# Holding a rotation's copies behind products, and a nearer norm broadcast, in a two-layer hybrid block

## The chip, the cores and the metric

One core of a Trainium2 chip runs the kernel. The metric is the device time of one execution in microseconds. All times below are from the kernel before: its timed runs and one profiled execution.

## What is computed

Two layers over 512 tokens of width 1024, in float32. Each layer projects the normalised input to many parts, mixes them in three branches, and adds a feed-forward part and a gated part:

```python
h = rms_norm(x, g_pre_mix)
q, k, v, qi, ki, wi, xr, gr, zu, zv, gate_logits = jnp.split(h @ w_in, offsets, axis=-1)
q, k, qi, ki = (apply_partial_rope(a, positions, 16) for a in (q, k, qi, ki))   # written out one by one
y_a = dsa_attention(q, k, v, qi, ki, wi)     # scores of qi, ki, wi select 128 keys of 512
y_b = rg_lru(causal_depthwise_conv(xr, ...), ...) * gelu(gr)
y_c = chunked_spatial_gating(gelu(zu), rms_norm(gelu(zv), g_gmlp_v), ...)
merged = jnp.einsum('bsnd,nbsd->bsd', sigmoid(gate_logits), branches_of(y_a, y_b, y_c))
x = x + rms_norm(merged @ w_out, g_post_mix)
x = x + rms_norm(square(relu(rms_norm(x, g_pre_ffn) @ w_ffn_up)) @ w_ffn_down, g_post_ffn)
x = x + rms_norm((p_i @ w_ple) * sigmoid(x @ w_ple_gate), g_post_ple)
```

`apply_partial_rope` is the rotation: it turns the first 16 of each head's 64 columns by the position.

## The kernel before

**Products.** Every float32 product is made of three with the operands split in a high and a low part (`mm3`, L298 to L300; L590 in `tokens`; L356 in `gemm_arriving`): `wh` by `xh`, `wl` by `xh`, `wh` by `xl`. The 303 weight tiles of 128x1024 come by DMA from the SP queue. `prep` makes `wh` with a cast on ScalarE (ACT, L243) and `wl` with a subtraction on VectorE (DVE, L244), three tiles ahead of TensorE (PE) and with four buffers each. A tile is 24 products of 512 columns.

**Rotations.** `rope` takes a projection from PSUM: on DVE a multiplication (L573) and a shuffle (L574), then on GpSimd (POOL) a multiplication (L575) and an addition (L576). What follows a rotation is the split of its result: `ki_split`, `stacked` (L650 on ACT, L651 on DVE, in pairs) for `qi` and `k`, `q_split` (L1026, L1028 on ACT, L1027 on DVE) for `q`. `xc_split` (L616 on ACT, L617 on POOL) does the same for the convolution's result, which is not rotated.

**What sets the order.** The program is traced against a clock `clk` that only products advance (`tick`). `defer(us, fn)` puts `fn` on a list, and `run_later` traces it when the clock has passed `us` more microseconds. So `defer(TURN, ...)` traces a split 5 us of product time after its projection. Tasks on `idxq` (indexer: scores L681, then a selection of MAX8 and MATCH_REPLACE8, L714 and L716) and `attq` (attention) give their steps in the same way. Behind this the Tile framework's scheduler puts the instructions of each engine in order, by their dependencies. A copy can therefore land ahead of products or weight splits that were traced before it.

**Norms.** `rstd_tok` sums the squares with small products (L408), then DVE (L427) and POOL (L428) make 1/rms per token. `rstd_bc` spreads it over the partitions with transposes (L434). `Stats.row` and `Norm.complete` defer the first by 2.2 us after the last square and the second by 3.0 us more. In both layers `R`, the spread 1/rms, scales the projections; `x_tiles` uses it for the residual (L480 to L503).

**Attention.** `turn` transposes two blocks of the softmax's result (L953), splits them (L369 on ACT, L370 on DVE), and `values` multiplies them by V (L967).

Of the kernel before, what the change touches and what calls it, by code (L numbers as in the profile page):

```python
# [17 lines left out]
S = 512  # L18
# [27 lines left out]
def f32v(ap):  # L46
    return ap.bitcast(F32)
# [3 lines left out]
def hybrid_block_kernel(ctx, tc, xT, pT, pos, vec, bsp, freq, w_in, w_tok, w_lru, w_sp, w_br, w_out, w_up, w_dn, w_ple, w_gate, out, depth=DEPTH, dbg=None):  # L51
    nc = tc.nc
    V, A, G, PE = nc.vector, nc.scalar, nc.gpsimd, nc.tensor
# [13 lines left out]
    def tmp(dt=F32):  # L67
        return tp.tile([128, S], dt, tag="tmp", name=nm("tmp"), bufs=NTMP)
# [4 lines left out]
    def bank():  # L73
        return pp.tile([128, 512], F32, tag="ps", name=nm("ps"), bufs=8)

    def slot(tag, dt=F32, big=False):
        return cp.tile([128, 4, S] if big else [128, S], dt, tag=tag, name=nm(tag))
# [10 lines left out]
    TAIL = 3  # L88
    LEAD = 256
    ATT = 13  # L90
    TURN = 5
    WARM = 120
    FIRST = [0, 1, 4]

# [152 lines left out]
    def getw(key, ahead=LA):  # L247
        assert order[nget[0]][0] == key, (order[nget[0]][0], key)
        nget[0] += 1
        while nprep[0] < min(nget[0] + ahead, len(order)):  # L250
            prep()
        return prepared.pop(key)
# [8 lines left out]
    def defer(us, fn):  # L261
        later.append((clk[0] + us, uid[0], fn))
        uid[0] += 1

    def run_later(force=False):
        while later:
            later.sort(key=lambda e: e[:2])
            if not force and later[0][0] > clk[0]:
                return
            later.pop(0)[2]()  # L270

    def add_task(q, gen):
        q["wait"].append(gen)
# [17 lines left out]
    def finish(q):  # L291
        run_later(force=True)
        while q["act"] or q["wait"]:
            tick(0.3)
# [7 lines left out]
    def gemm(ps, w, xs, kk, c0=0, st=None, r=FULL):  # L302

        h3, l3 = [v.rearrange("p (k c) -> p k c", k=kk) for v in w]
        for k in range(kk):
            if st is not None and k == kk - 2:
                st.partial()
            mm3(ps, h3[:, k, c0:c0 + 128], l3[:, k, c0:c0 + 128], xs[k][0][:, r], xs[k][1][:, r], k == 0, k == kk - 1)
            tick(0.65 * width(r) / S)
# [67 lines left out]
    class Stats:  # L377
# [59 lines left out]
        def row(self, div, dst):  # L437


            def complete(r):  # L440
                def tok():
                    self.rstd_tok(div, r)
                    defer(3.0, lambda: A.copy(dst[:, r], self.rstd_bc(r)))

                defer(2.2, tok)

            return complete

    class Norm:
# [6 lines left out]
        def complete(self, r):  # L456
            def tok():
                self.st.rstd_tok(self.div, r)
                defer(3.0, bc)

            def bc():
                self.gens[r.start] = self.tiles(r, self.st.rstd_bc(r))

            defer(2.2, tok)
# [68 lines left out]
    for l in range(depth):  # L533
        vc = vecs[l]

        def col(c):
            return vc[:, c:c + 1]
# [18 lines left out]
        def proj(name, ahead=LA):  # L556
            ps = bank()
            gemm(ps, getw(("in", l, name), ahead), XS, KT)
            return ps
# [11 lines left out]
        def rope(ps, n=128):  # L571
            t1, u = tmp(), tmp()
            V.tensor_mul(t1[:n], ps[:n], Cr[:n])  # L573
            V.stream_shuffle(u[:n], ps[:n], mask=SHUF)  # L574
            G.tensor_mul(u[:n], u[:n], Sr[:n])  # L575
            G.tensor_add(t1[:n], t1[:n], u[:n])  # L576
            return t1
# [19 lines left out]
        idxq = {"wait": [], "act": [], "max": 1}  # L597
# [5 lines left out]
        for j in range(4):  # L603
            ps = first[j]
            xr = tmp()
            V.tensor_mul(xr, ps, R)
            xc = slot(f"M{4 + j}")
            A.activation(xc, xr, AF.Identity, bias=col(V_CB + j), scale=col(V_CW + 12 + j))
            for i in range(3):
                s = 3 - i  # L610
                V.scalar_tensor_tensor(xc[:, s:], xr[:, :S - s], col(V_CW + 4 * i + j), xc[:, s:], op0=ALU.mult, op1=ALU.add)
            xh, xl = slot(f"B{j}", F32R), slot(f"B{4 + j}", F32R)
            XC.append((xc, xh, xl))

            def xc_split(xc=xc, xh=xh, xl=xl):
                A.copy(xh, xc)  # L616
                G.tensor_sub(xl, xc, f32v(xh))  # L617

            defer(10 + 5 * j, xc_split)


        ps = proj("ki")
# [5 lines left out]
            A.copy(kih[64:128], kf[0:64])  # L628
            A.copy(kil[64:128], f32v(kil[0:64]))

        defer(TURN, ki_split)
        wf = tmp()
        A.copy(wf, ps)
        WI = small(32, "wi", 2).rearrange("p (t h) -> p t h", t=4)
# [5 lines left out]
            for t in range(1, 4):  # L640
                V.tensor_scalar(WI[:, t, :], pw[:, t * 128 + 64:t * 128 + 72], rt[:, t:t + 1], IDX_SCALE, op0=ALU.mult, op1=ALU.mult)

        defer(9, wi_turn)

        def stacked(f, q0, q1):


            for s, q in enumerate((q0, q1)):
                r, other = slice(64 * s, 64 * s + 64), slice(64 - 64 * s, 128 - 64 * s)
                A.copy(q[r], f[r])  # L650
                V.tensor_sub(q[other], f[r], f32v(q[r]))  # L651
            return q0, q1

        QI = []
        for j in range(4):
            ps = proj(f"qi{j}")
            QI.append((slot(f"A{j}", F32R), slot(f"A{4 + j}", F32R)))
            defer(TURN, lambda f=rope(ps), q=QI[j]: stacked(f, *q))

        def qk(a, b, c, d, jobs):  # L660

# [23 lines left out]
        def scores(t, sc):  # L685
            n = 128 * (t + 1)
            qs = slice(t * 128, (t + 1) * 128)
            for j in range(4):
                pr = qk_full(QI[j], kih, kil, t, n)
                for s in range(2):  # L690
                    rl = tmp()
                    A.activation(rl[:, :n], pr[s][:, :n], AF.Relu)
                    w = WI[:, t, 2 * j + s:2 * j + s + 1]
                    if j == 0 and s == 0:
                        V.tensor_scalar(sc[:, :n], rl[:, :n], w, None, op0=ALU.mult)
                    else:
                        V.scalar_tensor_tensor(sc[:, :n], rl[:, :n], w, sc[:, :n], op0=ALU.mult, op1=ALU.add)
                yield 3.4
            V.tensor_add(sc[:, qs], sc[:, qs], tri)

        def indexer():
            sc = {t: tmp() for t in (1, 2, 3)}
            for t in (1, 2, 3):
                yield from scores(t, sc[t])
            for t in (1, 2, 3):
                yield from select(t, sc[t])
# [23 lines left out]
            G.tensor_scalar(BIAS[t], gt[:, :n], -NEG, NEG, op0=ALU.mult, op1=ALU.add)  # L730
            yield 1.0

        defer(9, lambda: add_task(idxq, indexer()))


        bs = tmp()
# [23 lines left out]
        for j in range(4):  # L760
            ps = proj(f"zu{j}")
# [16 lines left out]
        for j in range(4):  # L778
# [3 lines left out]
            for hf in range(2):  # L782
                ps = bank()
# [4 lines left out]
                for s in range(2):  # L788
                    r = slice(64 * s, 64 * s + 64)
# [55 lines left out]
        for j in range(4):  # L845
# [7 lines left out]
            r, i = tmp(), tmp()  # L853
# [48 lines left out]
        def gated(n, ys, first=None, ds=range(8)):  # L902
            for d in ds:
                th = first if first is not None and d == 0 else gate(n, d)
                if d % 2 == 0:
                    w = getw(("br", l, n, d // 2), ahead=1)
                branch(n, d, w, ys, th)
# [5 lines left out]
        KK = [slot("K0", F32R, True), slot("K1", F32R, True)]  # L913
# [105 lines left out]
        for j in range(4):  # L1019
            f = rope(proj(f"q{j}"))  # L1020
            q2, ql = (slot(f"A{j}", F32R), slot(f"A{4 + j}", F32R)), tmp(F32R)

            def q_split(f=f, q2=q2, ql=ql):
                for s in range(2):
                    r, other = slice(64 * s, 64 * s + 64), slice(64 - 64 * s, 128 - 64 * s)
                    A.copy(q2[s][r], f[r])  # L1026
                    V.tensor_sub(ql[r], f[r], f32v(q2[s][r]))  # L1027
                    A.copy(q2[s][other], f32v(q2[s][r]))  # L1028

            defer(TURN, q_split)  # L1030
            Q.append((q2, ql))
            defer(TURN, lambda f=rope(proj(f"k{j}")), j=j: stacked(f, KK[0][:, j], KK[1][:, j]))
            if j == 0:
                finish(idxq)
            defer(ATT, lambda j=j: add_task(attq, attention(j)))
            gated(1, YB, ds=range(2 * j, 2 * j + 2))
# [23 lines left out]
        for d in range(5):  # L1060
            ps = bank()
# [8 lines left out]
        ps = bank()  # L1070
# [52 lines left out]
        for c in range(2):  # L1123
            w = getw(("ple", l, c), ahead=1)
            if c == 1:
                bc = st3.rstd_bc()
            for i in range(4):
                ps = bank()
# [14 lines left out]
        for d in range(5):  # L1143
            if d < 4:
                ps = first[d]
            else:
                ps = bank()
# [95 lines left out]
```

## Time and profile before

| | us |
|---|---|
| median of 3 runs | 1851.07 (1850.51 to 1853.98) |
| profiled execution | 1852.94 |
| its span in the profile | 1851.2 |
| PE busy | 1803.0 |
| DVE busy | 1159.5 |
| ACT busy | 800.3 |
| POOL busy | 361.6 |

Busy time is a mean over stages that differ: DVE's 63% holds a stretch of 120 us in which it hardly idles. PE's records overlap, since its products are pipelined: what counts is the distance from the start of one to the start of the next. A number in brackets at the end of a row is the idle time of the engine just before that instruction, with the instruction whose result ended it.

### The profile page before, as it was taken

The numbers are of one execution on the slowest core, as the hardware profiler recorded it, in microseconds if no ns is written. First come the engines' busy times: TensorE is split into PE (matmuls) and PEld (weight loads), VectorE is DVE, ScalarE is ACT, GpSimd is POOL, SyncE is SP. The second block draws the span as 40 slices with busy tenths as digits, with TensorE's granted clock in tenths as the row PEclk, the third lists the DMA queues.
The fourth block names the chain that finished last, engine by engine and source line by source line (L and its number), as shares of the span: only waits on it lengthen the run. The fifth ranks groups of instructions, "written<-read, shape, count | busy, mean of one in ns | idle before, by whom it ended". The sixth has DMA issues, their size and how long they took to land.

```text
span 1851.2 us, 22873 instructions
## 1 busy us (share of the span) xinstructions
PE 1803.0 (97%) x8798; PEld 1507.5 (81%) x8798; DVE 1159.5 (63%) x1939; ACT 800.3 (43%) x1292; POOL 361.6 (20%) x292
## 2 busy tenths in 40 slices
PE   8899999999999999999998999999999999999997
PEld 7787887888888888888887878877888888888886
DVE  6689996666386253533685999866563852544355
ACT  5466435664453322223455573455544432222233
POOL 3513212210240000003454141222004200000033
PEclk9999999999999999999999999999999999999999
DMA  5122322222223232332212223222222222222321
GB/s 173 63 92 85 98 92 91 69 80 82 90 80 108 97 98 96 99 106 91 92 58 97 68 92 103 91 80 72 89 80 92 92 92 101 96 97 97 108 80 58
DMA packets 49678, 167.77 MB, mean 91 GB/s; under 512 B 6048, under 2 KB 8864, under 8 KB 49568
## 3 DMA queue, kind: packets, MB, share of 16 engines
q1 hardware_dynamic: 47376, 163.64, 26.8%
q10 hardware_dynamic: 2192, 2.67, 0.4%
q8 instruction: 69, 1.13, 0.3%
q14 instruction: 41, 0.34, 0.1%
HBM read 164.19 MB, written 2.10 MB: 90 GB/s over the span
## 4 chain that ended last, share of the span: by engine, by line
PE 72%; DVE 12%; POOL 6%; issue 6%; ACT 4%; DMA 0%; SPq 0%; POOLq 0%; DVEq 0%; ACTq 0%
PE ps L298 21%; PE ps L299 20%; PE ps L300 20%; PE ps L356 3%; PE ps L590 3%; DVE wl L244 2%; POOL tmp L575 1%; POOL tmp L576 1%; DVE tmp L716 1%; DVE m L714 1%; POOL sacc L398 1%; POOL X L483 1%; PE ps L681 1%; PE ps L967 1%; DVE tmp L790 1%
## 5 line engine op out<-in xcount | busy, mean ns | idle before, releaser
L243 ACT CAST wh<-wr 128x1024 fp32r<-128x1024 f32 x303 | 316.6, 1049 | 453.3 <-PE ps L300 365.9
L244 DVE TENSOR_TENSOR wl<-wr,wh 128x1024 fp32r<-128x1024 f32 x303 | 386.8, 1280 | 188.7 <-ACT wh L243 188.0
L298 PE MATMUL ps<-xh,wh 128*128 128x512 f32 (+1 forms) x1296 | 502.7, 388 | 0.9 <-DVE tmp L370 0.9
L299 PE MATMUL ps<-xh,wl 128*128 128x512 f32 (+1 forms) x1296 | 495.5, 382 | 3.0 <-DVE wl L244 3.0
L300 PE MATMUL ps<-xl,wh 128*128 128x512 f32 (+1 forms) x1296 | 495.6, 382 | 0.0
L398 POOL TENSOR_TENSOR sacc<-sacc,tmp 128x256 f32<-128x256 f32 (+1 forms) x99 | 109.8, 1109 | 894.8 <-issue 584.5
L300 PEld LDWEIGHTS ps<-xl,wh 128*128 128x128 f32 x1296 | 243.9, 188 | 48.2
L299 PEld LDWEIGHTS ps<-xh,wl 128*128 128x128 f32 x1296 | 244.4, 189 | 47.1 <-DVE wl L244 3.9
L298 PEld LDWEIGHTS ps<-xh,wh 128*128 128x128 f32 x1296 | 244.0, 188 | 47.2 <-issue 1.9
L300 PE MATMUL ps<-V,wh 128*128 128x512 f32 (+1 forms) x528 | 195.4, 370 | 0.0
L298 PE MATMUL ps<-K,wh 128*128 128x512 f32 (+1 forms) x432 | 158.2, 366 | 0.0
L299 PE MATMUL ps<-K,wl 128*128 128x512 f32 (+1 forms) x432 | 157.8, 365 | 0.0
L300 PE MATMUL ps<-B,wh 128*128 128x512 f32 x336 | 130.9, 390 | 0.0
L298 PE MATMUL ps<-A,wh 128*128 128x512 f32 x320 | 125.0, 391 | 0.2 <-ACT A L369 0.2
L299 PE MATMUL ps<-A,wl 128*128 128x512 f32 x320 | 124.6, 389 | 0.0
L1102 DVE TENSOR_TENSOR M<-M,ps 128x512 f32<-128x512 f32 x48 | 33.0, 688 | 141.4 <-PE ps L300 141.4
L300 PEld LDWEIGHTS ps<-V,wh 128*128 128x128 f32 x528 | 99.5, 188 | 16.7
L1090 DVE TENSOR_TENSOR tmp<-ps,R 128x512 f32<-128x512 f32 x64 | 43.8, 690 | 108.6 <-PE ps L300 108.5
L356 PE MATMUL ps<-xl,wh 128*128 128x256 f32 (+1 forms) x264 | 88.1, 334 | 6.2 <-DVE xl L503 5.5
L298 PEld LDWEIGHTS ps<-K,wh 128*128 128x128 f32 x432 | 81.5, 189 | 13.3
L299 PEld LDWEIGHTS ps<-K,wl 128*128 128x128 f32 x432 | 81.5, 189 | 13.1
L356 PE MATMUL ps<-xh,wh 128*128 128x256 f32 (+1 forms) x264 | 87.1, 330 | 2.2 <-ACT xh L493 2.2
(237 smaller groups left out, 2733.0 us busy)
## 6 DMA issues: line engine op xcount, KB each, us to landing
wr<-in_w_in_dram SPq DMA_DIRECT2D x95, 512.0 KB, 3.3
wr<-in_w_up_dram SPq DMA_DIRECT2D x64, 512.0 KB, 3.3
wr<-in_w_dn_dram SPq DMA_DIRECT2D x64, 512.0 KB, 3.3
wr<-in_w_br_dram SPq DMA_DIRECT2D x24, 512.0 KB, 3.3
wr<-in_w_tok_dram SPq DMA_DIRECT2D x16, 512.0 KB, 3.3
wr<-in_w_out_dram SPq DMA_DIRECT2D x16, 512.0 KB, 3.3
wr<-in_w_gate_dram SPq DMA_DIRECT2D x16, 512.0 KB, 3.3
X<-in_xT_dram SPq DMA_DIRECT2D x8, 256.0 KB, 5.9
```

The costliest lines, as they stand in the source:

```text
L243: A.copy(hi, raw)
L244: V.tensor_sub(lo, raw, f32v(hi))
L298: PE.matmul(ps, wh, xh, start=start, stop=False)
L299: PE.matmul(ps, wl, xh, start=False, stop=False)
L300: PE.matmul(ps, wh, xl, start=False, stop=stop)
L356: PE.matmul(pss[o][:, r], (h3, l3, h3)[m][:, q], xs[q][m // 2][:, r], start=q == 0 and m == 0, stop=q == KT - 1 and m == 2)
L398: G.tensor_add(sacc[:, r], sacc[:, r], self.q[r.start, r.stop])
L483: (G if d in on_g else V).tensor_add(X[d][:, r], X[d][:, r], ys[d][:, r])
L575: G.tensor_mul(u[:n], u[:n], Sr[:n])
L590: PE.matmul(ps, x, w, start=k == 0 and i == 0, stop=k == KT - 1 and i == 2)
L1090: V.tensor_mul(t, ps, R)
L1102: V.tensor_add(F[d], F[d], ps)
```

## The change

Two numbers change and one is new: `TURN` 5 to 7, and `PICK` 1.7 in place of the 3.0 us between a norm's statistics and its broadcast. A new helper, `behind_products`, traces a function and gives each instruction that it made on ACT, DVE or POOL a dependency for the scheduler alone (no semaphore) on the last PE instruction traced before. `turn_later` is `defer` with that helper, and the splits behind rotations and `xc_split` use it. Some delays change: `xc_split` 10 to 12, `wi_turn` 9 to 14, the start of the indexer 9 to 12, and the statistics of the first half in `row` 2.2 to 8.0.

```diff
-    TURN = 5
+    TURN = 7
+    PICK = 1.7
...
+    def behind_products(fn):
+        ins = nc.cur_bb.bb.instructions
+        n0 = len(ins)
+        mark = next(i for i in reversed(ins[:n0]) if i.engine == mybir.EngineType.PE)
+        fn()
+        for i in nc.cur_bb.bb.instructions[n0:]:
+            if i.engine in (mybir.EngineType.Activation, mybir.EngineType.DVE, mybir.EngineType.Pool):
+                tc.add_manual_dep(i, mark.name, mybir.DependencyInfo(mybir.DependencyClass.NoSync, mybir.DependencyReason.SCHED_ONLY), reason="behind products")
+
+    def turn_later(us, fn):
+        defer(us, lambda: behind_products(fn))
...
-                    defer(3.0, lambda: A.copy(dst[:, r], self.rstd_bc(r)))
-                defer(2.2, tok)
+                    defer(PICK, lambda: A.copy(dst[:, r], self.rstd_bc(r)))
+                defer(2.2 if r.stop == S else 8.0, tok)
...
-                defer(3.0, bc)
+                defer(PICK, bc)
...
-            defer(10 + 5 * j, xc_split)
+            turn_later(12 + 5 * j, xc_split)
...
-        defer(TURN, ki_split)
+        turn_later(TURN, ki_split)
...
-        defer(9, wi_turn)
+        defer(14, wi_turn)
...
-            defer(TURN, lambda f=rope(ps), q=QI[j]: stacked(f, *q))
+            turn_later(TURN, lambda f=rope(ps), q=QI[j]: stacked(f, *q))
...
-        defer(9, lambda: add_task(idxq, indexer()))
+        defer(12, lambda: add_task(idxq, indexer()))
...
-            defer(TURN, q_split)
+            turn_later(TURN, q_split)
...
-            defer(TURN, lambda f=rope(proj(f"k{j}")), j=j: stacked(f, KK[0][:, j], KK[1][:, j]))
+            turn_later(TURN, lambda f=rope(proj(f"k{j}")), j=j: stacked(f, KK[0][:, j], KK[1][:, j]))
```

In the orders below the changed kernel's lines have other numbers: L244 is L245, L573 and L574 are L589 and L590, L575, L576 and L617 are L591, L592 and L633, L641 and L651 are L657 and L667, and L369, L1026, L1028 are L384, L1042, L1044.

On DVE in layer 0, behind the weight of the first tokens tile: `wl_129` (now `wl_128`), `wl_138` and `wl_151` are those of the second, third and fourth, and `A0` to `A7` are the rotated `qi`. Before (`wl_151` follows, behind the shuffle that belongs to the last row):

```order
L651 TENSOR_TENSOR A0_111_642<-tmp_113_644,A0_111_642 64x512
L651 TENSOR_TENSOR A4_112_643<-tmp_113_644,A4_112_643 64x512
L574 STREAM_SHUFFLE tmp_124_697<-ps_116_650 128x512
L244 TENSOR_TENSOR wl_129_706<-wr_127_703,wh_128_705 128x1024
L573 TENSOR_TENSOR tmp_132_741<-ps_126_702,tmp_73_523 128x512
L574 STREAM_SHUFFLE tmp_133_742<-ps_126_702 128x512
L651 TENSOR_TENSOR A1_121_694<-tmp_123_696,A1_121_694 64x512
L651 TENSOR_TENSOR A5_122_695<-tmp_123_696,A5_122_695 64x512
L244 TENSOR_TENSOR wl_138_751<-wr_136_748,wh_137_750 128x1024
L651 TENSOR_TENSOR A2_130_739<-tmp_132_741,A2_130_739 64x512
L651 TENSOR_TENSOR A6_131_740<-tmp_132_741,A6_131_740 64x512
L573 TENSOR_TENSOR tmp_141_786<-ps_135_747,tmp_73_523 128x512
```

Now:

```order
L245 TENSOR_TENSOR wl_128_693<-wr_126_690,wh_127_692 128x1024
L667 TENSOR_TENSOR A0_111_636<-tmp_113_638,A0_111_636 64x512
L667 TENSOR_TENSOR A4_112_637<-tmp_113_638,A4_112_637 64x512
L657 TENSOR_SCALAR wi_105_604<-ps_129_720,rt_37_283 128x8 x3
L589 TENSOR_TENSOR tmp_132_735<-ps_125_689,tmp_73_523 128x512
L590 STREAM_SHUFFLE tmp_133_736<-ps_125_689 128x512
L245 TENSOR_TENSOR wl_138_745<-wr_136_742,wh_137_744 128x1024
L667 TENSOR_TENSOR A1_120_681<-tmp_122_683,A1_120_681 64x512
L667 TENSOR_TENSOR A5_121_682<-tmp_122_683,A5_121_682 64x512
L589 TENSOR_TENSOR tmp_141_780<-ps_135_741,tmp_73_523 128x512
L590 STREAM_SHUFFLE tmp_142_781<-ps_135_741 128x512
L245 TENSOR_TENSOR wl_151_795<-wr_149_792,wh_150_794 128x1024
```

Each of the three weights stands ahead of one pair more than before, and the `wi` step, which stood ahead of the rows before, stands behind the first pair.

On POOL in the same place, up to the addition that ends the rotation of `qi1` (`tmp_123_696`, now `tmp_122_683`); `B4` to `B7` are the convolution's low parts. Before:

```order
L617 TENSOR_TENSOR B4_78_535<-M4_76_529,B0_77_534 128x512
L617 TENSOR_TENSOR B5_83_544<-M5_81_538,B1_82_543 128x512
L617 TENSOR_TENSOR B6_88_553<-M6_86_547,B2_87_552 128x512
L575 TENSOR_TENSOR tmp_100_595<-tmp_100_595,tmp_74_524 64x512
L576 TENSOR_TENSOR tmp_99_594<-tmp_99_594,tmp_100_595 64x512
L617 TENSOR_TENSOR B7_93_562<-M7_91_556,B3_92_561 128x512
L575 TENSOR_TENSOR tmp_114_645<-tmp_114_645,tmp_74_524 128x512
L576 TENSOR_TENSOR tmp_113_644<-tmp_113_644,tmp_114_645 128x512
L575 TENSOR_TENSOR tmp_124_697<-tmp_124_697,tmp_74_524 128x512
L576 TENSOR_TENSOR tmp_123_696<-tmp_123_696,tmp_124_697 128x512
```

Now:

```order
L591 TENSOR_TENSOR tmp_100_595<-tmp_100_595,tmp_74_524 64x512
L633 TENSOR_TENSOR B4_78_535<-M4_76_529,B0_77_534 128x512
L592 TENSOR_TENSOR tmp_99_594<-tmp_99_594,tmp_100_595 64x512
L591 TENSOR_TENSOR tmp_114_639<-tmp_114_639,tmp_74_524 128x512
L592 TENSOR_TENSOR tmp_113_638<-tmp_113_638,tmp_114_639 128x512
L633 TENSOR_TENSOR B5_83_544<-M5_81_538,B1_82_543 128x512
L591 TENSOR_TENSOR tmp_123_684<-tmp_123_684,tmp_74_524 128x512
L592 TENSOR_TENSOR tmp_122_683<-tmp_122_683,tmp_123_684 128x512
```

The low parts `B6` and `B7` moved behind the rotation of `qi1`, and `B5` behind that of `qi0`.

On ACT in layer 0, at the first `turn` of the attention (`tmp_547`, `tmp_550`, `tmp_561`) and the second `q` (`A1`, `A5`). Before:

```order
L1026 CAST A1_537_2636<-tmp_535_2630 64x512
L1026 CAST A5_538_2637<-tmp_535_2630 64x512
L369 CAST tmp_547_2664<-ps_546_2659 128x512
L1028 CAST A1_537_2636<-A1_537_2636 64x512
L1028 CAST A5_538_2637<-A5_538_2637 64x512
L243 CAST wh_558_2703<-wr_557_2701 128x1024
L369 CAST tmp_550_2690<-ps_549_2686 128x384
```

Now:

```order
L384 CAST tmp_547_2664<-ps_546_2659 128x512
L244 CAST wh_558_2697<-wr_557_2695 128x1024
L384 CAST tmp_550_2684<-ps_549_2680 128x384
L1042 CAST A1_537_2636<-tmp_535_2630 64x512
L1042 CAST A5_538_2637<-tmp_535_2630 64x512
L1044 CAST A1_537_2636<-A1_537_2636 64x512
L1044 CAST A5_538_2637<-A5_538_2637 64x512
```

The two splits of turned logits and a weight's cast stand ahead of the four copies of `q1`.

## Rows read from the trace of the kernel before

**Rows 1.** The page's first part: each engine's busy us, share of the span, instructions.

```profile
PE 1803.0 (97%) x8798; PEld 1507.5 (81%) x8798; DVE 1159.5 (63%) x1939; ACT 800.3 (43%) x1292; POOL 361.6 (20%) x292
```

**Rows 2.** PE's waits: who waited for what, us in total, times, longest.

```profile
PE ps L590 <- DVE wl L244: 10.5, 4, 4.2
...
PE ps L299 <- DVE wl L244: 4.4, 4, 1.5
PE ps L967 <- ACT tmp L369: 4.1, 4, 2.3
...
PE ps L967 <- DVE tmp L370: 1.7, 4, 0.9
...
PE ps L639 <- ACT tmp L633: 1.2, 2, 0.7
```

**Rows 3.** PE's timeline at the tokens of layer 0: start, us, instruction, idle before.

```profile
70.76 0.39 PE L590 MATMUL ps<-wh,xl 128*128 128x512 f32 x1
72.24 0.50 PE L590 MATMUL ps<-wl,xh 128*128 128x512 f32 x1 [1.09 <-DVE wl L244]
72.57 0.40 PE L590 MATMUL ps<-wh,xh 128*128 128x512 f32 x1
...
74.86 0.39 PE L590 MATMUL ps<-wh,xl 128*128 128x512 f32 x1
79.46 0.80 PE L590 MATMUL ps<-wl,xh 128*128 128x512 f32 x1 [4.21 <-DVE wl L244]
```

**Rows 4.** DVE's timeline at the same place.

```profile
68.86 1.41 DVE L651 TENSOR_TENSOR A<-tmp,A 64x512 fp32r<-64x512 f32 x2 [3.45 <-ACT A L650]
...
75.38 2.76 DVE L651 TENSOR_TENSOR A<-tmp,A 64x512 fp32r<-64x512 f32 x2 [1.93 <-ACT A L650]
78.18 1.23 DVE L244 TENSOR_TENSOR wl<-wr,wh 128x1024 fp32r<-128x1024 f32 x1
```

**Rows 5.** ACT's timeline at the same place.

```profile
68.21 1.26 ACT L650 CAST A<-tmp 64x512 fp32r<-64x512 f32 x2 [3.87 <-POOL tmp L576]
```

**Rows 6.** Stretches of layer 0: length, busy us (PE, PEld, DVE, ACT, POOL), PEclk, DMA.

```profile
52.00:79.40 27.40, 21.70 (x95) 17.02 (x93) 17.45 (x28) 10.14 (x16) 19.09 (x11) 0.96 0.18 61
79.40:84.00 4.60, 4.54 (x11) 3.62 (x12) 3.82 (x7) 0.56 (x1) 1.71 (x1) 0.50 0.48 158
84.00:104.00 20.00, 20.00 (x97) 16.89 (x96) 11.08 (x20) 14.54 (x29) 3.86 (x4) 1.00 0.34 106
...
130.00:250.00 120.00, 117.82 (x534) 97.54 (x534) 115.30 (x218) 60.25 (x77) 32.39 (x24) 1.00 0.26 84
```

**Rows 7.** The same for a stretch of layer 1.

```profile
994.00:998.50 4.50, 4.32 (x10) 3.45 (x11) 3.95 (x7) 0.68 (x1) 1.48 (x1) 0.50 0.57 173
```

**Rows 8.** PE's timeline at two gates and branches of layer 0.

```profile
179.24 0.50 PE L299 MATMUL ps<-xh,wl 128*128 128x512 f32 x1 [1.52 <-DVE wl L244]
...
201.95 0.50 PE L299 MATMUL ps<-V,wl 128*128 128x512 f32 x1 [0.66 <-DVE wl L244]
```

**Rows 9.** ACT's timeline at the first turn of layer 0's attention.

```profile
293.47 1.26 ACT L1026 CAST A<-tmp 64x512 fp32r<-64x512 f32 x2 [4.60 <-POOL tmp L576]
```

**Rows 10.** PE's timeline at the same place.

```profile
295.39 0.50 PE L967 MATMUL ps<-tmp,V 128*128 128x256 f32 x2 [1.15 <-ACT tmp L369]
```

**Rows 11.** PE's timeline at the norm behind the output projection, layer 0.

```profile
506.08 0.38 PE L434 MATMUL ps<-ident,rt 128*128 128x128 f32 x2
```

**Rows 12.** POOL's timeline at the same norm.

```profile
502.82 0.71 POOL L428 TENSOR_TENSOR rt<-sm,mhalf 128x2 f32<-128x2 f32 x1 [1.84 <-DVE sm L427]
```

**Rows 13.** POOL's timeline just ahead of the rotations of layer 0.

```profile
53.95 4.11 POOL L617 TENSOR_TENSOR B<-M,B 128x512 fp32r<-128x512 f32 x1 [1.34 <-ACT B L616]
```

**Rows 14.** POOL's groups from 50 to 84 us: shapes, count, busy us, mean ns, idle.

```profile
L617 POOL TENSOR_TENSOR B<-M,B 128x512 fp32r<-128x512 f32 x4 | 10.4, 2604 | 9.8 <-ACT B L616 9.8
L575 POOL TENSOR_TENSOR tmp<-tmp,tmp 128x512 f32<-128x512 f32 x4 | 7.1, 1763 | 7.5 <-DVE tmp L574 7.5
L576 POOL TENSOR_TENSOR tmp<-tmp,tmp 128x512 f32<-128x512 f32 x3 | 4.2, 1385 | 0.2
```

## The prediction

> **What bounds the kernel now.** I read the busy times first. TensorE (PE) is busy for 1803.0 of 1851.2 us and DVE for 1159.5 [rows 1], so little can come from doing less: what can come is the time in which PE stands. The second view is PE's waits [rows 2]. The largest one is L590, the products of `tokens`, on `wl`, the low part of a weight that DVE makes: 10.5 us in four waits. Then come L299 on `wl` (4.4) and the attention's L967 on L369 and L370 (4.1 and 1.7). The third view is the place of the largest wait, layer 0 between 70 and 80 us [rows 3]. Products follow each other every (74.86 - 72.57) / 10 = 0.229 us; one stands from 70.76 to 72.24, so 1.25 us are lost, and one from 74.86 to 79.46, so 4.37 are lost.
>
> Why is `wl` late? DVE runs in order, and its `wl` at 78.18 stands behind the L651 pair of a rotated `qi`, which starts only at 75.38 [rows 4]. L651 waits for ACT's L650, and L650 waits for POOL's L576, the last step of the rotation [rows 5]. So a weight that needs no rotation waits for a rotation. DVE idles 3.45 and 1.93 us in front of two such pairs, with `wl` behind them that it could have made. The wait costs twice: in the 4.60 us after it the granted clock is 0.50, which is the 1.2 GHz level, and 11 products run there [rows 6]. At 0.229 they take 2.5 us, so 2.1 are lost. With about 0.6 for L639 on L633 (1.2 in two waits [rows 2]) layer 0 loses 1.25 + 4.37 + 2.1 + 0.6 = 8.3 us at this place. Layer 1 has the other two of the four waits, and after them a stretch of 4.50 us at 0.50 with 10 products [rows 7], 2.2 lost; I take 8.3 for it too.
>
> **Part 1: rotations behind products.** `behind_products` adds no instruction and no semaphore wait. It forbids the scheduler to put a rotation's copies on ACT, DVE or POOL ahead of the product traced just before them, and `TURN` 5 to 7 traces them 2 us of product time later. The order shows what comes of it on DVE: of the four tokens weights the second `wl`, which stood behind the first L651 pair, stands ahead of it; the third, behind two pairs, now stands behind one, and the fourth, behind three, behind two. What each waits for now: the third for the rotation of `qi0`, whose L650 starts at 68.21 in the trace [rows 5] and can start sooner with one L617 ahead of it on POOL where there were four; the fourth for that of `qi1`. The `wi` step stands in front of the third too, but its products come before the `qi2` that the third follows anyway. Walking the new order with the durations of the rows, I get the third `wl` at about 68.5 where PE needs it at 72.5, and the fourth at 73 to 74 against 75.2 (four products of each of three kinds per tile, 12 x 0.229 = 2.7 us apart). Nothing waits, though the fourth has little over 1 us to spare. What is late next in that place is nothing I can find: L639 moves some 5 us of products back, well behind the copy that it waited for. So 8.3 per layer, 16.6 us, are saved; the bounds are 0 (the wait moves to another pair) and 8.8 (all that PE loses there).
>
> Does the lead last? From 52 to 104 us DVE idles 27.40 - 17.45, 4.60 - 3.82 and 20.00 - 11.08, in sum 19.7 us, so it has room to run 8 us ahead. From 130 to 250 it is busy for 115.3 of 120 [rows 6], so there PE goes no faster than DVE, and PE's lead at the end is at most DVE's. The work on DVE is the same, so a DVE that enters that stretch 8 us sooner leaves it 8 us sooner, unless another engine's result makes it wait: it waits for 4.7 us in the 120. In that stretch PE waits 1.52 and 0.66 for `wl` [rows 8]. In the new order the first of these `wl` stands ahead of six MAX8 and MATCH_REPLACE8 of the indexer's selection and of two L869 that wait for POOL, some 7 us of DVE work, and the second some 6 earlier. Both waits should go, but DVE then owes that work a little later. Of 2 x 2.2 us I count 1.2 per layer, 2.4 (from 0 to 4.4).
>
> **Part 2: attention.** In layer 0 ACT's first L369, the split of the first turned logits, stands behind L1026, the `q` copy, which waited 4.60 us for POOL [rows 9]; PE's L967 waits for it [rows 10]. In the new order two L369 stand ahead of that L1026, and their L370 ahead of L1027. L967 loses 4.1 + 1.7 = 5.8 us in all [rows 2]; I count 4.5, since in later rounds the copy now stands behind softmax steps and may hold a turn that it didn't hold. Bounds 0 and 5.8.
>
> **Part 3: norms.** `PICK` 3.0 to 1.7 traces the broadcast L434 twelve 256-column products sooner in the halves, about 1.4 us. At 506.08 [rows 11] that is 504.6, and its input is ready at 502.82 + 0.71 = 503.5 [rows 12], so it doesn't wait. But the two `wl` and `xl` steps that follow stand in DVE's order, and PE gets back perhaps 0.5 of each such place; against it the row statistics of the first half (2.2 to 8.0) put their small products elsewhere. At the very end there is nothing behind which the chain could hide: the last L427 moves ahead of an L482 and L483 pair, worth 0.5. I count 2 us for all norms, between -1.5 and 4: the smallest of the terms, and the one I trust least.
>
> **New waits.** Some pieces come later by design: the scores, the selection, the copies of `k`. I subtract 2.5 us, two waits like the first in [rows 10] (1.15), between 0 and 7.
>
> **The sum.** 16.6 + 2.4 + 4.5 + 2 - 2.5 = 23.0 us. The profiled execution took 1852.94 us (span 1851.2), which is 1.87 above the median of the runs, 1851.07. So the profiled one would give 1829.9 and the median **1828 us**.
>
> **Rivals.**
> *A. DVE gives the lead back.* If the rotations come so late that DVE holds its lead only partly in the stretch from 130 to 250, where it is busy 96% of the time [rows 6], then PE's gain at the first place turns into small waits for `wl` there. For it: two `wl` are late there already [rows 8]. Against it: the same work, started sooner. With 3 us kept per layer: 2 x 3 + 4.5 + 2 = 12.5, about 1839 us.
>
> *B. Slower: POOL becomes the bound of the rotations.* L617, which stood three in a row ahead of all rotations and once more behind `ki`'s, is now spread between them. One POOL pass at 53.95 took 4.11 us [rows 13]; the mean of L617 here is 2.6, that of L575 1.76, of L576 1.39 [rows 14]. Until `qi1` is rotated the new order has eight POOL passes from about 54 us on (two L617 and three each of L575 and L576). At the means of the rows they take 2 x 2.6 + 3 x 1.76 + 3 x 1.39 = 14.7 us and end near 69. The weight cast on ACT behind the `qi1` copies, the copies and the `wl` need another 3.5, so 72 against 75.2. If DVE, which now idles less, slows every pass to 4.11, they end at 86.8, the fourth `wl` is 15 us late, and with 2 more for the clock each layer loses 8.8 us more than now; less 4.5 + 2 from the other parts the kernel is some 11 us slower, about 1862. It decides from a mean pass of about 3.4 us, double what the rows give. The Trainium skill, GPSIMD Engine Reference, section 8 (Key points), speaks for this rival: GpSimd shares its SBUF interfaces with VectorE and contends with VectorE instructions that have two SBUF inputs. It gives no price; what it would make of the sum is B's time. The trace agrees as far as passes over the same 128x512 range from a mean of 1.39 to 4.11 us.
>
> *C. Nothing moves.* The clock stretches and the waits shift by some us but stay, since one wait is exchanged for another everywhere: 1851. Against it is the order, in which the pairs do move.
>
> **Chances.** The forecast (a gain of over 14 us) 0.64, A 0.18, B 0.09, C 0.09. What a measurement here can tell from no change is about 0.2%, 3.7 us. Faster by more than that 0.82, within it 0.09, slower 0.09. The range reaches to A's case and leaves out B and C: at the low end 2 x 8.8 + 4.4 + 5.8 + 4 with no new waits is 32 us, 1819; at the high end 1843, where A keeps 1 us per layer.
>
> **What would show it.** Right: no wait of L590 for `wl`, and a granted clock of 1.00 from 70 to 84 us; the L681 scores about 5 us sooner; PE about 9 us ahead at 250, 12 at 500 and 20 to 24 at the end. Wrong on the lead: DVE without idle time up to 250 and more waits of L299 on `wl`. Wrong by B: L575, L576 and L617 above 3 us and L650 still waiting for L576, with `wl` behind it. Wrong on attention: L967 waits as long as before, for other L369. The forecast fails most easily if DVE's order after 104 us, which I read piece by piece, holds a wait for ACT or POOL that I have not seen.

## The result and the profile after

The changed kernel takes 1830.53 us (median of 4 runs, 1827.38 to 1831.04) against 1850.85 before: a ratio of 0.988 (0.987 to 0.990), 20.3 us less. The forecast was 1828. Its profiled execution has a span of 1828.8 us, 22.4 less than before. The lines of the page's first part and of PE's waits that answer [rows 1] and [rows 2]:

```profile
PE 1793.8 (98%) x8798; PEld 1503.6 (82%) x8798; DVE 1169.1 (64%) x1939; ACT 796.0 (44%) x1288; POOL 364.4 (20%) x292
```

```profile
PE ps L314 <- DVE wl L245: 10.5, 6, 3.3
PE ps L371 <- DVE xl L519: 8.0, 9, 3.8
PE ps L423 <- ACT tmp L407: 2.0, 1, 2.0
PE ps L449 <- POOL rt L443: 1.9, 2, 1.1
```

The numbers of lines are those of the changed file: L314 is L299, L606 is L590, L983 is L967, L245 is L244. The largest wait of before, L590's 10.5 us on `wl`, has no row any more, nor have L967's. But L299's on `wl` grew from 4.4 in four waits to 10.5 in six. The stretches of layer 0 that answer [rows 6], with the same columns:

```profile
52.00:79.40 27.40, 27.40 (x124) 22.68 (x123) 23.91 (x32) 12.35 (x20) 24.41 (x14) 1.00 0.33 108
79.40:84.00 4.60, 4.60 (x24) 3.88 (x23) 2.97 (x5) 4.48 (x7) 0.84 (x1) 1.00 0.00 0
84.00:104.00 20.00, 20.00 (x97) 16.93 (x96) 15.46 (x32) 16.95 (x33) 2.13 (x2) 1.00 0.37 121
...
130.00:250.00 120.00, 114.68 (x501) 93.98 (x501) 110.63 (x208) 57.44 (x75) 30.04 (x22) 0.99 0.27 89
```

From 52 to 104 us PE stands nowhere and its granted clock is 1.00; DVE is busy for 42.35 us there instead of 32.35. From 130 to 250 PE is busy for 3.1 us less than before, and DVE for 4.7 less.

The table says where the time went in each profiled execution. A number is PE's lost time in a stretch: the distances between the starts of successive products, less the median distance of products of the same shape, in us. The columns are named by what stands there: the tokens (50 to 100 us in layer 0, and the same place in layer 1), the gates and the recurrence (150 to 250), the attention (250 to 475), the norms behind the output projection, the layers' border, the end. Two layers are joined by a plus. The first 50 us are left out: there the programs hardly differ, and single executions lost 4.4 to 8.1.

| kernel | median | tokens | gates | attention | norms | border | end |
|---|---|---|---|---|---|---|---|
| before | 1850.85 | 8.8 + 9.0 | 2.6 + 2.9 | 9.5 + 9.9 | 3.2 + 3.1 | 7.5 | 4.1 |
| after | 1830.53 | 0.1 + 0.1 | 7.6 + 7.8 | 3.8 + 3.4 | 2.5 + 2.4 | 6.6 | 3.5 |
| indexer at 9 | 1819.20 | 0.2 + 0.2 | 2.6 + 2.6 | 3.8 + 4.5 | 2.5 + 2.4 | 6.5 | 3.0 |
| indexer at 15 | 1834.99 | 0.1 + 0.0 | 10.6 + 9.2 | 3.8 + 5.3 | 2.5 + 2.5 | 6.6 | 3.5 |
| half the selection | 1825.97 | 0.2 + 0.1 | 7.0 + 7.2 | 3.4 + 3.5 | 2.5 + 2.4 | 6.6 | 3.0 |
| no helper | 1851.10 | 6.7 + 6.8 | 7.5 + 7.8 | 8.3 + 8.0 | 2.5 + 2.5 | 6.6 | 3.5 |
| TURN 5 | 1845.10 | 9.3 + 8.5 | 7.5 + 7.8 | 4.0 + 3.4 | 2.5 + 2.5 | 6.6 | 3.1 |
| helper alone | 1839.72 | 8.8 + 7.3 | 2.6 + 2.8 | 5.4 + 3.8 | 3.2 + 3.1 | 7.7 | 4.1 |
| indexer at 9, norms undone | 1832.55 | 3.8 + 4.0 | 2.6 + 2.8 | 3.8 + 4.5 | 3.2 + 3.1 | 7.8 | 4.1 |
| indexer at 9, TURN 6 | 1819.25 | 0.2 + 0.2 | 2.6 + 2.7 | 3.8 + 4.5 | 2.5 + 2.4 | 6.4 | 3.0 |
| indexer at 9, row undone | 1822.48 | 0.2 + 0.2 | 2.6 + 2.6 | 3.8 + 4.5 | 3.7 + 3.6 | 6.7 | 3.3 |

So the change gained 17.7 us at the tokens, 12.1 in the attention and 2.9 at norms, border and end, and lost 9.9 at the gates (differences of the numbers before rounding). That is 22.8 in sum; the start lost 0.4 more than before, which leaves the 22.4 of the spans.

### The profile page after: what moved, and what is told of

Same layout as the page of the kernel before. It is cut to its first block, busy times and chain, and to the rows that moved or that the text cites. A ratio compares the mean times of both kernels' runs of the same rounds, so it can differ in the third digit from the quotient of the medians.

```text
span 1828.8 us, 22863 instructions
## 1 busy us (share of the span) xinstructions
PE 1793.8 (98%) x8798; PEld 1503.6 (82%) x8798; DVE 1169.1 (64%) x1939; ACT 796.0 (44%) x1288; POOL 364.4 (20%) x292
## 4 chain that ended last, share of the span: by engine, by line
PE 84%; DVE 7%; issue 3%; POOL 3%; ACT 3%; DMA 0%; SPq 0%; ACTq 0%; POOLq 0%; DVEq 0%
PE ps L313 24%; PE ps L315 24%; PE ps L314 24%; PE ps L606 5%; PE ps L371 4%; DVE wl L245 1%; PE ps L983 1%; DVE tmp L732 1%; PE ps L969 1%; DVE m L730 1%; PE ps L697 1%; POOL sacc L413 1%; POOL X L499 1%; DVE xl L519 1%; PE ps L683 1%
## 5 line engine op out<-in xcount | busy, mean ns | idle before, releaser
L244 ACT CAST wh<-wr 128x1024 fp32r<-128x1024 f32 x303 | 317.9, 1050 | 464.8 <-PE ps L315 380.8
L314 PE MATMUL ps<-xh,wl 128*128 128x512 f32 (+1 forms) x1296 | 496.8, 383 | 10.5 <-DVE wl L245 10.5
L245 DVE TENSOR_TENSOR wl<-wr,wh 128x1024 fp32r<-128x1024 f32 x303 | 385.6, 1275 | 185.8 <-ACT wh L244 185.4
L313 PE MATMUL ps<-xh,wh 128*128 128x512 f32 (+1 forms) x1296 | 503.6, 389 | 0.0
L314 PEld LDWEIGHTS ps<-xh,wl 128*128 128x128 f32 x1296 | 244.8, 189 | 56.5 <-DVE wl L245 13.0
L313 PEld LDWEIGHTS ps<-xh,wh 128*128 128x128 f32 x1296 | 244.5, 189 | 46.0 <-issue 1.9
L313 PE MATMUL ps<-K,wh 128*128 128x512 f32 (+1 forms) x432 | 158.2, 366 | 0.0
L314 PE MATMUL ps<-K,wl 128*128 128x512 f32 (+1 forms) x432 | 157.8, 365 | 0.0
L313 PE MATMUL ps<-A,wh 128*128 128x512 f32 x320 | 125.0, 391 | 0.2 <-ACT A L384 0.2
L314 PE MATMUL ps<-A,wl 128*128 128x512 f32 x320 | 124.6, 389 | 0.0
L313 PEld LDWEIGHTS ps<-K,wh 128*128 128x128 f32 x432 | 81.4, 189 | 13.2
L314 PEld LDWEIGHTS ps<-K,wl 128*128 128x128 f32 x432 | 81.5, 189 | 13.1
```

Of the source, the lines that this page charges most:

```text
L244: A.copy(hi, raw)
L245: V.tensor_sub(lo, raw, f32v(hi))
L313: PE.matmul(ps, wh, xh, start=start, stop=False)
L314: PE.matmul(ps, wl, xh, start=False, stop=False)
```

## Experiments: what took the lead back at the gates

PE comes to the gate g2_3 10.1 us sooner than before, waits there for `wl`, waits twice more, and leaves the stretch 3.4 us sooner. The row on PE, and DVE's rows ahead of it:

```profile
177.16 0.39 PE L313 MATMUL ps<-xh,wh 128*128 128x512 f32 x1
180.82 0.79 PE L314 MATMUL ps<-xh,wl 128*128 128x512 f32 x1 [3.28 <-DVE wl L245]
```

```profile
164.55 1.49 DVE L245 TENSOR_TENSOR wl<-wr,wh 128x1024 fp32r<-128x1024 f32 x1 [2.44 <-ACT wh L244]
168.29 1.77 DVE L885 SCALAR_TENSOR_TENSOR B<-tmp,B 128x512 f32<-128x512 f32 x1 [2.25 <-POOL tmp L884]
...
179.55 1.22 DVE L245 TENSOR_TENSOR wl<-wr,wh 128x1024 fp32r<-128x1024 f32 x1
```

DVE idles 2.44 us for a cast that stands behind sigmoids on ACT, and 2.25 us for POOL's step of the recurrence (L884), with the `wl` of g2_3 behind it in line. From 169.99 us on DVE hardly idles up to that `wl`: it makes up steps of the recurrence and of the selection. The cast that this `wl` needs ended at 172.35 + 1.03 = 173.38, so for 6 us it could have been made and stood in line:

```profile
172.35 1.03 ACT L244 CAST wh<-wr 128x1024 fp32r<-128x1024 f32 x1
```

The wait costs the clock too: the granted clock is 0.61 from 181 to 185 us, with 12 products in 4 us. At 0.39 x 4.00 that is 1.6 us of the 7.6 lost per layer; the three waits are 3.4, 1.5 and 0.9, as distances.

```profile
181.00:185.00 4.00, 4.00 (x12) 3.14 (x13) 3.67 (x6) 3.99 (x6) 3.02 (x3) 0.61 0.43 133
```

**The indexer's start.** It is the one part of the change that moves the selection.

```diff
-        defer(12, lambda: add_task(idxq, indexer()))
+        defer(9, lambda: add_task(idxq, indexer()))
```

> The changed kernel with the indexer's start back at 9 us (from 12). In it DVE's order from 130 to 250 us is that of the kernel before, all else is of the changed one. Theory 1 (the lead of 10 us that PE has at 177 us is lost because the later start puts the weight splits of g2_3, g2_5 and g2_7 behind recurrence and selection steps): the waits of 3.4, 1.5 and 0.9 us per layer go, those of before (1.5 and 0.7) may stay, PE keeps 7 to 9 us per layer and the time is about 1821 us (1818 to 1825). Theory 2 (DVE is full from 130 to 250 us, the lead is lost in any order): 1829 to 1832 us, with waits of the same sum for other weights.

Measured: 1819.20 us (ratio to before 0.9825, 0.981 to 0.984). At the gates 2.6 us are lost per layer, as before the change, and little else moves (one product of layer 1's attention waits 1 us). Theory 1 holds, and the delay of 12 costs the change 11 us. This is the best kernel of the study (with TURN 6 on top it takes the same, see below). The stretches from 160 to 170 us, of after and of this run:

```profile
160.00:170.00 10.00, 10.00 (x46) 8.29 (x45) 4.76 (x7) 9.94 (x14) 6.17 (x6) 1.00 0.16 55
```

```profile
160.00:170.00 10.00, 8.50 (x38) 6.75 (x37) 8.52 (x17) 9.74 (x14) 4.94 (x5) 1.00 0.00 0
```

DVE is busy for 4.76 us in the one and 8.52 in the other. With the start at 9 the selection's steps stand between the recurrence's steps and fill DVE's waits for POOL; at 12 they stand elsewhere. DVE's rows of this run show what is left of the waits, and three weights made in a row:

```profile
163.78 1.76 DVE L885 SCALAR_TENSOR_TENSOR B<-tmp,B 128x512 f32<-128x512 f32 x1 [1.24 <-POOL tmp L884]
...
168.43 4.33 DVE L245 TENSOR_TENSOR wl<-wr,wh 128x1024 fp32r<-128x1024 f32 x3
```

From 104 to 250 us DVE idles for 12.8 of 146 us in the changed kernel and for 7.0 in this run. That speaks most directly against theory 2: the changed kernel doesn't lack DVE time there, but an order that uses it. ACT is full from 160 to 170 us in both (9.94 and 9.74 of ten), so a full ACT doesn't explain the difference either.

> The changed kernel with the indexer's start at 15 us. In DVE's order nearly every weight split from g2_2 to q0 stands 3 to 8 us of work further ahead than in the kernel before; the selection comes later. Theory 1 (order decides): the waits of 3.4, 1.5 and 0.9 us per layer go, about 1819 us (1815 to 1824), unless the attention's logits now wait for the selection, which would show as a wait of PE at the first logits of 2 us or more. Theory 2 (DVE full in any order): 1829 to 1833 us.

Measured: 1834.99 us, 10.6 + 9.2 lost at the gates. Both theories miss: it is not that weights further ahead are better. Here they stood so far ahead that one waited for ACT's cast itself (a wait of 1.2 us on `wh`, then 2.6 and 3.3 on `wl`).

**Is DVE short of time?** The selection cut to 8 rounds (this kernel selects 64 keys, not 128):

```diff
-            for r in range(TOPK // 8):
+            for r in range(TOPK // 16):
-                if r < TOPK // 8 - 1:
+                if r < TOPK // 16 - 1:
```

> The changed kernel (indexer at 12) with 8 rounds of the selection instead of 16 per block of queries, so it selects 64 keys: DVE has some 24 us less to do per layer. Theory 1 (the weight splits come late because DVE is full and idles in the wrong place just before): the waits at g2_3, g2_5 and g2_7, 3.4, 1.5 and 0.9 us, mostly go, and with them 10 us: 1818 to 1822 us. Rival (the splits wait for ACT and POOL in front of them, whatever DVE has to do): g2_3 still waits about 2 to 3.5 us, 1825 to 1830 us.

Measured: 1825.97 us (one run), 7.0 + 7.2 still lost at the gates. The rival holds, at a neighbouring weight. The time alone would not say so: of the 4.6 us that it is faster than the changed kernel, 2.5 lie in the start and 1.2 at the gates. DVE is busy for 6.44 us of the ten from 160 to 170, and in front of the late `wl` it idles for POOL:

```profile
160.00:170.00 10.00, 8.10 (x36) 6.41 (x35) 6.44 (x4) 9.94 (x15) 8.33 (x6) 1.00 0.04 6
```

```profile
163.56 3.21 DVE L885 SCALAR_TENSOR_TENSOR B<-tmp,B 128x512 f32<-128x512 f32 x2 [4.21 <-POOL tmp L884]
166.69 4.04 DVE L245 TENSOR_TENSOR wl<-wr,wh 128x1024 fp32r<-128x1024 f32 x2
```

So less load on DVE doesn't cure it. The order differs in this kernel too, so it is weaker evidence than the run with the indexer at 9, and it points the same way. It is the pattern of the tokens again: a weight in line behind a step of another chain, here the recurrence's, which waits for POOL and ACT.

## Experiments: what frees the tokens and the attention

**Without the helper**, with all the new delays (`defer(us, fn)` in `turn_later`):

> The changed kernel with turn_later as plain defer: later delays, but no scheduler dependency. The weight split of the fourth tokens tile stands behind three rotated pairs again, that of the third behind two rotated pairs less a step. Theory 1 (the delay of 7 us does most of it): tokens wait for wl at one or two places, 1 to 3 us per layer, time 1832 to 1838 us. Rival (the dependency does it): the waits of the kernel before come back in full, 5.6 us and the low clock behind them, 1844 to 1848 us.

Measured: 1851.10 us (0.9999, 0.999 to 1.001): no gain. The tokens keep 6.7 + 6.8 and the attention 8.3 + 8.0. Theory 1 falls. The rival's waits come back, less at the tokens than before; the time is 3 us over its range, and it had left out what the gates lose with the indexer at 12 (7.5 + 7.8 against 2.6 + 2.9). A form of wait that before did not show stands first at the tokens, the cast on ACT behind the `qi` copies:

```profile
PE ps L606 <- ACT wh L244: 5.2, 2, 2.6
PE ps L606 <- DVE wl L245: 3.5, 4, 1.5
```

**With the helper but the old delay:**

```diff
-    TURN = 7
+    TURN = 5
```

> The changed kernel with TURN back at 5, the helper and all other delays kept. Theory 1 (the delay does it): tokens wait for wl of the third and fourth tile as before, 4 to 8 us per layer with the clock, and L967 waits in the attention again, 1843 to 1850 us. Rival (the helper does it): 1829 to 1833 us.

Measured: 1845.10 us. The tokens lose 9.3 + 8.5 (PE's waits there are 7.1 us for `wh`, behind the `qi` copies on ACT, and 3.1 for `wl`), the attention 4.0 + 3.4. Theory 1 holds at the tokens, the rival in the attention: there the helper is enough.

**The helper alone**, all numbers as before the change:

> The kernel before with the helper alone: turn_later at the old delays (5, 10 + 5 j), and PICK 3.0, row 2.2, wi 9, indexer 9 as before. Theory 1 (the helper frees the attention, the tokens need the longer delay as well): waits of L967 on L369 gone, about 11 us saved there, the tokens' waits stay: 1840 us (1837 to 1844). Rival (the helper works only together with the delay, as in the tokens): 1850 us.

Measured: 1839.72 us. Theory 1 holds: the attention's waits of L967 are gone (one product L313 in layer 0 still waits 1.3 us for L385, the L370 of before) and the tokens' stay, in one wait per layer:

```profile
PE ps L606 <- DVE wl L245: 10.8, 2, 5.7
```

**TURN 6**, on the kernel with the indexer at 9:

> As the run with the indexer at 9 us, with TURN 6 in place of 7. DVE's order at the tokens and from 130 to 250 us is that of TURN 7; only the split of k2 stands differently. Theory 1 (time follows the order): 1818 to 1821 us. Rival (the delay itself counts, half the tokens' waits come back): 1826 us or more.

Measured: 1819.25 us. Time follows the order, which is that of TURN 7 at the tokens.

**The norms undone**, on the same kernel:

```diff
-    PICK = 1.7
+    PICK = 3.0
-                defer(2.2 if r.stop == S else 8.0, tok)
+                defer(2.2, tok)
```

> As the run with the indexer at 9 us, with the norms as before (PICK 3.0, row 2.2). Theory 1 (the norm part is worth about 2 to 3 us: 0.7 at each norm of the middle, 0.9 at the layers' border, 0.6 to 1 at the end): 1821 to 1823 us against 1819.2. Rival (the norm part gives nothing): 1819 us.

Measured: 1832.55 us, 13.4 more; both theories miss. Norms, border and end lose 3.8 more, somewhat over theory 1's 2 to 3; but the tokens lose 3.8 + 4.0, which neither had. The first norm of a layer makes `R`, and every rotation waits for `R`. ACT's copies of `R`, of this run and of the one with the indexer at 9:

```profile
39.80 1.05 ACT L244 CAST wh<-wr 128x1024 fp32r<-128x1024 f32 x1 [4.74 <-PE ps L315]
40.76 0.58 ACT L458 COPY R<-ps 128x512 f32<-128x512 f32 x1
```

```profile
38.26 0.59 ACT L458 COPY R<-ps 128x512 f32<-128x512 f32 x1 [4.44 <-PE ps L449]
39.00 1.05 ACT L244 CAST wh<-wr 128x1024 fp32r<-128x1024 f32 x1 [0.16 <-PE ps L315]
```

With PICK 1.7 `R` is copied ahead of a weight's cast, not behind it. By the rows it starts 2.5 us sooner, but 1.2 of that is the start of the two executions (PE's first L313 product is at 33.06 us in the one and 31.81 in the other); counted from there it is 1.3 us, 0.7 from the earlier broadcast and 0.6 from the cast. The fourth `wl` of the tokens has little to spare in after (it ends at 74.48 + 1.21 = 75.69, and PE's first product with it starts at 76.15); without the early `R` it is late, and PE waits 3.9 us for `wl` at L606 in two waits.

**Only row undone:**

> As the run with the indexer at 9 us, with only the statistics of a first half in row back at 2.2 us (PICK stays 1.7). Undoing both cost 13 us. Theory 1 (PICK does it: R comes sooner, so the rotations do too): 1818 to 1821 us. Rival (the 8.0 of row does it): 1826 us or more.

Measured: 1822.48 us, 1.5 over theory 1's range. The tokens stay free, so it is PICK that frees them. The 8.0 of `row` is worth 2.5 to 3 us, at the norms (3.7 + 3.6 against 2.5 + 2.4): at 2.2 the small products stand among those of `gemm_arriving`, and the broadcast L449 waits 1.8 us for POOL's 1/rms in each layer.

## Experiments: can the recurrence be held back as well?

If the gates suffer from the same pattern, the same helper might cure it. Each step of the recurrence's task through `behind_products`, with the indexer at 12 and at 9, and then all tasks:

```diff
-                        a[0] = clk[0] + next(a[1])
+                        us = [None]
+                        if "behind" in q:
+                            behind_products(lambda: us.__setitem__(0, next(a[1], None)))
...
-        recq = {"wait": [recurrence()], "act": [], "max": 1}
+        recq = {"wait": [recurrence()], "act": [], "max": 1, "behind": 1}
```

> The changed kernel (indexer at 12) with each step of the recurrence (L881 to L900 of the changed file) traced through behind_products as well, so that its instructions on ACT, DVE and POOL can't stand ahead of the product traced before them. In DVE's order the weight splits of g2_2 to g2_5 stand 6 to 11 us of work further ahead than in the kernel before. Theory 1 (these splits are late because they stand behind recurrence steps that wait for POOL and ACT): the waits at g2_3, g2_5 and g2_7 go, PE keeps its lead of 8 to 10 us per layer: 1813 to 1820 us. Rival (a later recurrence makes PE wait for its result at the branch products, or DVE is short of time all the same): 1826 us or more.

> The same with the indexer at 9 us. Theory 1: the waits of 1.7 and 0.8 us per layer that are left at g2_2 and the branch go as well, 1812 to 1817 us. Rival: a new wait at the branch of the recurrence's result, 1820 us or more.

> As the run with the indexer at 9 us, with the steps of all tasks (indexer, attention, recurrence) traced through behind_products. Theory 1 (work that no product needs soon should never stand ahead of a weight split): 1812 to 1818 us. Rival (the selection or the softmax then comes too late and PE waits for it at the logits or at L983): over 1820 us, with waits at those lines.

Measured: 1849.43, 1843.69 and 1859.72 us. Theory 1 falls in all three and the times are the rivals', but the waits are not quite those that they named. At the gates 7.5 + 7.8, 7.7 + 7.2 and 7.0 + 6.5 are lost, and PE waits there for weights, not for the recurrence's result: in the second, the `wl` at 196.14 us, whose cast ended at 191.31, stands behind a scan of the recurrence (L902), a step of the selection and two of the gates. In the attention 14.9 + 15.6, 10.2 + 14.3 and 19.9 + 19.9 are lost. PE's largest waits of the second and third:

```profile
PE ps L321 <- DVE wl L245: 9.7, 4, 4.0
...
PE ps L990 <- ACT tmp L391: 4.7, 5, 1.4
```

```profile
PE ps L320 <- DVE tmp L860: 15.5, 2, 7.7
PE ps L321 <- DVE wl L245: 9.1, 2, 4.6
```

In the third, PE waits 7.7 us per layer for a gate's multiplication on DVE (L860), which stands behind the selection's last steps. In the first two POOL's last pass of the recurrence in layer 0 ends at about 201 us, and the attention's larger waits stand at 293 us and from 426 on, so they don't come from its steps standing in line there. PE's own order has changed: its last product of `values` in layer 0 starts 13 to 14 us behind the last product of the gates, against 1.1 in the changed kernel, so that the last turns have no product to hide behind. How a dependency on the recurrence's steps leads to that order isn't shown.

## Why the prediction was right, point by point

**Tokens: right in size, half right in cause.** 16.6 us were counted and 17.7 came. The walk through the new order was close: the third `wl` was put at 68.5 and starts at 68.60, the fourth at 73 to 74 and starts at 74.48. In DVE's timeline of after that answers [rows 4]:

```profile
68.60 1.20 DVE L245 TENSOR_TENSOR wl<-wr,wh 128x1024 fp32r<-128x1024 f32 x1
...
74.48 1.21 DVE L245 TENSOR_TENSOR wl<-wr,wh 128x1024 fp32r<-128x1024 f32 x1
```

The low clock behind the wait went with it, as counted. But the text gave the gain to the helper and the delay. It takes at least three parts at once: the helper (without it 6.7 + 6.8 are lost), the delay (8.5 to 9.3 at 5 us; 6 will do) and PICK (3.8 + 4.0 without the norms' part, a test with the indexer at 9). Whether the delays of `xc_split` and `wi_turn` are needed as well no run shows; they were never undone alone.

**Gates: wrong, by 12 us.** Counted was a gain of 2.4, measured a loss of 9.9. The step that failed is "Both waits should go" and the sentence before it, that DVE keeps its lead "unless another engine's result makes it wait". Both weights that had waited did move ahead; the wait went to g2_3, g2_5 and g2_7, and DVE did wait, for ACT and POOL. Nor did the term hold the low clock behind the first of these waits. The prediction's own sign shows it: PE was to be 9 us ahead at 250 us, 12 at 500 and 20 to 24 at the end, and was 3.4, 9.0 and 22.4. The prediction had named this as the way in which it would fail most easily. Rival A named the outcome (3 us kept per layer; 3.4 were) but gave a full DVE as its reason; the run with the indexer at 9, where DVE has the same work and the lead stays, and the run with half the selection speak against it.

**Attention: right in mechanism, too small by 7.6 us.** Counted were 4.5 with 5.8 as the bound; 12.1 came. The term held only the waits of L967, and those as PE's idle time, 5.8 us; as distances between starts, by which the tokens were counted, the same eight waits are 7.0. The longest of them also costs the clock, as at the tokens: in layer 1 of the kernel before, the stretches behind the wait of 2.3 us have this granted clock:

```profile
1212.30:1216.00 3.70, 3.55 (x12) 2.80 (x13) 3.66 (x7) 1.49 (x2) 0.00 (x0) 0.72 0.01 2
1216.00:1220.00 4.00, 4.00 (x21) 3.18 (x20) 1.20 (x2) 0.56 (x1) 2.56 (x2) 0.83 0.40 131
```

At 0.28 x 3.70 and 0.17 x 4.00 that is 1.7 us. The shorter waits of layer 0, up to 1.2 us, cost no clock; it stays at 1.00 there:

```profile
290.00:300.00 10.00, 7.34 (x37) 5.50 (x36) 5.15 (x9) 4.98 (x8) 3.35 (x2) 1.00 0.29 98
300.00:310.00 10.00, 9.10 (x48) 7.19 (x48) 6.68 (x18) 4.37 (x10) 2.59 (x2) 1.00 0.31 107
```

With 1.1 for a product (L298) that waits for L370, also as a distance, the parts that can be named come to 9.8; the other 2.3 lie in waits of 0.4 us or less each.

**Norms: 2 counted, 2.9 measured directly**, inside the bounds. What they do for the tokens was not in the term.

**New waits: 2.5 counted.** None came in the attention; those at the gates are in the term above.

**Rival B fell.** POOL's passes of after that answer [rows 14]:

```profile
L633 POOL TENSOR_TENSOR B<-M,B 128x512 fp32r<-128x512 f32 x4 | 7.5, 1869 | 0.8 <-ACT B L632 0.8
L591 POOL TENSOR_TENSOR tmp<-tmp,tmp 128x512 f32<-128x512 f32 x4 | 7.4, 1845 | 1.0 <-DVE tmp L590 1.0
L592 POOL TENSOR_TENSOR tmp<-tmp,tmp 128x512 f32<-128x512 f32 x4 | 6.6, 1654 | 0.2
```

The means are 1.65 to 1.87 us, far from the 3.4 at which it would decide. The total came out within 3 us because the errors nearly cancel: -12.3 at the gates against +7.6 in the attention, +2.5 for new waits that were counted and didn't come, and +2.0 at tokens and norms. That the sum is so close is luck.

## What to carry over

Where one queue in order makes weights and also serves a chain over other engines, look at each place where a weight stands behind a step of that chain; the waits of the weight's reader show only the one that ends last. Holding a chain back behind products is no cure in general: it freed the rotations, and applied to the recurrence as well it cost 19 and 24 us, most of it in the attention, where PE's order had changed as well. A delay that moves work past a stretch should be tried alone: here one of six numbers (TURN, PICK and four delays) cost 11 of the 31 us that the helper and the other five gained.

## What the runs showed of the hardware

DVE and POOL slow each other down. In the kernel before a pair of L651 took 1.41 us while POOL idled and 2.76 while it worked [rows 4]; in the changed one, with POOL's passes from 63.09 to 68 us beside it, the pair took 3.36 us for the same work:

```profile
63.57 3.36 DVE L667 TENSOR_TENSOR A<-tmp,A 64x512 fp32r<-64x512 f32 x2
```

Beside this pair POOL's passes took 1.59 to 1.74 us against 1.28 alone. Beside a weight split it is the other way round. The `wl` at 68.60 us took its usual 1.20 us (shown above), and the POOL pass that started 0.2 us behind it took 2.18:

```profile
68.78 2.18 POOL L591 TENSOR_TENSOR tmp<-tmp,tmp 128x512 f32<-128x512 f32 x1 [0.70 <-DVE tmp L590]
```

So neither engine always pays. In these rows the one that started later did: the L591 pass ends 1.16 us behind the `wl`, which is nearly a whole pass. No run was made to test that. Rival B's sentence from the Trainium skill (GPSIMD Engine Reference, section 8, Key points) says that the two share interfaces; the trace agrees, with the times above.
